# The last quarter of both MLPs' down products in seven quarter products, with part of the preparation on GpSimd

## The chip, the core and the metric

The kernel runs on one core of one Trainium2 chip. The metric is the device time of one execution, in microseconds (us); lower is better. A core has five engines with a queue of instructions each, and every queue runs strictly in its own order: TensorE (PE in the profile; its weight loads are PEld), VectorE (DVE), ScalarE (ACT), GpSimd (POOL) and SyncE (SP, which here only issues DMAs). Engines wait for each other with semaphores. All operands come from SBUF, matmuls write to PSUM.

## The reference, cut to what matters

A two-layer decoder trunk on 512 tokens of width 1024, in float32. Layer 0 mixes with latent attention, layer 1 with sliding-window attention; each layer ends with a squared-relu MLP of inner width 4096 and a layer norm:

```python
def _mlp(x, w_up, w_down):
    h = jax.nn.relu(x @ w_up)
    return (h * h) @ w_down

x = _layernorm(alpha * x + mixer(x), ln_mix_g[l], ln_mix_b[l])
x = _layernorm(alpha * x + _mlp(x, w_up, w_down), ln_mlp_g[l], ln_mlp_b[l])
```

The change is only in `(h * h) @ w_down`, and in the layer norm that follows it, in both layers.

## The kernel before, in words

**Precision.** Every operand of a large product is held as two float32r tiles, a high part (ACT copies the value, line 77) and a low part (value minus high part, line 80, on DVE by default or on POOL). A product is three matmuls: high by high, high by low, low by high (`three`, line 108). A 128-row chunk of weights, 128 x 1024, so costs one DMA of 512 KB, one ACT instruction for `wh` and one low part `wl`.

**The stream of weights.** Line 112's `stream` lists all chunks in the order of their use. `weights` (line 307) hands out one chunk and prepares others up to four ahead, since the tags `wh` and `wl` have four buffers each. SP issues the DMAs in stream order.

**Seven products.** An up or down product of one block (1024 of the 4096 inner columns) is a 2 x 2 block product of quarters. `queue_seven` (line 166) and `Block` (line 715) do it with seven quarter products in place of eight, in the manner of Strassen and Winograd; products carry the numbers 1 to 7. The combinations of weights are made by DMA: product 1's quarter is loaded by SP (line 203), and once both parts of it are made, POOL issues a DMA that adds the next quarter onto the same tile (line 199). One tile (tag `quada` for down) so goes through products 1, 5, 6 and 4 in this order, another (`quadb`) through 3 and 7; product 2 has a plain load. Each tile has two halves. The combinations of activations are made by `Factors.sum` (line 618) on DVE, and `factor` (line 792) splits each into two parts in a tile of tag `fac`, three buffers. `u2` holds two 128 x 512 sums of products 1 and 6 that several outputs need; `take` and `add_plain` (lines 712 and 562) apply them to the residual tiles `xs` at the end.

**A down product** (`down_`, line 803) takes two token tiles t of 128 tokens, and per tile four inner chunks of three matmuls of 128 x 512: 24 matmuls a product.

**The order of the work** is written out by hand in line 39's `STEPS`: U stands for up, D for down, the prime for the next block. Blocks 0 to 2 run in this way. The last block (index 3, `NFF - 1`) has its up products in seven, but its down product is plain: `LAST_STEPS` (line 40) ends with D4 of block 2, then lines 857 to 877 make four factors and call `TokMajor.finish` (line 477). That does the left 512 columns of all four tiles, inner chunk by inner chunk, then the right 512 columns tile by tile: 24 matmuls a tile, and behind each the eviction, the layer norm (line 415: DVE statistics, POOL's power for the reciprocal root at line 398, two DVE instructions of 128 x 1024) and, in layer 0, the transposes of finished tiles (`turn_tokens`, line 430) for the next stage. Its eight chunks of weights are plain loads (line 277). Layer 0 goes on with `begin` (line 579), layer 1 writes the output (line 428).

A scheduler sets the order on DVE, ACT and POOL, except where `pe` and `pin` keep the program's order. PE keeps it throughout.

Of the kernel before, what the change touches and what calls it, by code (L numbers as in the profile page):

```python
# [9 lines left out]
F32R = mybir.dt.float32r  # L10
# [5 lines left out]
P = 128  # L16
D = 1024
# [7 lines left out]
NFF = 4  # L25
# [11 lines left out]
ON_POOL = ("w_h", "w_o", "w_sq", "w_so")  # L37

STEPS = "U'1 D5 U'2 D3 U'5 D6 D7 U'3 D4 U'6 U'7 U'4 D'1 D'2"
FIRST_STEPS, LAST_STEPS = "U'1 U'2 U'5 U'3 U'6 U'7 U'4 D'1 D'2", "U'1 D5 U'2 D3 U'5 D6 D7 U'3 U'6 U'7 U'4 D4"  # L40

AHEAD_S, AHEAD_B = 3, 2

# [5 lines left out]
def build(tc, nc, io, out):  # L49
    with ExitStack() as top:  # L50
# [112 lines left out]

        mlp_pool = [None]

        def queue_seven(name, key, chunk):

# [17 lines left out]
            def grown(a, jp, *more, aside=None):  # L185
                wh, wl = tiles_of_weights(aside)
                after = None
                if aside:
                    after = state.pop("plain", None)
                elif (key, a, jp, bool(more)) == ("U", "b", 0, True):  # L190
                    after = state.get("s4")
                elif (key, a, more) == ("U", "a", (1, 0)):
                    after = state.pop(("s2", jp), None)
                with behind(after):
                    state["last"] = split(
                        wh, wl, flat(half(a, jp)), keep=(a, bool(more)) == ("b", True) and key == "U"
                    )
                if more:
                    nc.gpsimd.dma_start(half(a, jp), chunk(*more, jp), accum_op=ALU.add)  # L199
# [81 lines left out]
        for m in range(2):  # L281
# [278 lines left out]
            pin(nc.vector.scalar_tensor_tensor(xs[t][:, c], xs[t][:, c], ALPHA, b, ALU.mult, ALU.add))  # L560

        def add_plain(t, c, b):
            nc.vector.tensor_add(xs[t][:, c], b, xs[t][:, c])  # L563

        def add_scaled_last(t, c, b):
            add_scaled(t, c, b)
# [41 lines left out]
        class Factors:  # L608

            def __init__(self, mp):
                self.mp = mp

            def scratch(self):
                return self.mp.tile([P, 4, 256], F32, tag="uv", bufs=3, name=nm("uv"))

            def sum(self, n, a11, a12, a21, a22):
                if n == 5:
                    self.a = self.scratch()  # L620
                    nc.vector.tensor_sub(self.a, a21, a22)
                    return self.a
                if n == 3:
                    nc.vector.tensor_sub(self.a, self.a, a11)
                    self.b = self.scratch()
                    nc.vector.tensor_add(self.b, a12, self.a)
                    return self.b
                if n == 7:
                    nc.vector.tensor_sub(self.b, a11, a21)
# [67 lines left out]
        def mlp(src, gb, dst, mp):  # L697
# [12 lines left out]
            own_bank = {1: 1, 2: 1, 5: 5, 7: 7, 4: 7, 6: 6}  # L710

            def take(t, c, b):
                nc.vector.tensor_sub(xs[t][:, c], xs[t][:, c], b)

            class Block:
                def __init__(self, q):
                    self.q = q
                    self.g = {}
                    self.banks = {}
                    self.down = Factors(mp)  # L720
                    self.fac = {}

                def bank(self, key, i):
# [65 lines left out]
                            nc.scalar.activation(self.g[done], self.g[done], AF.Square)  # L789


                def factor(self, n, quad=False):
                    if quad:
                        f = mp.tile([P, 2, 4, 256], F32R, tag="quada", bufs=1, name=nm("fac"))
                    else:
                        f = mp.tile([P, 2, 4, 256], F32R, tag="fac", bufs=3, name=nm("fac"))
                    g = [self.g.get(a) for a in ("a11", "a12", "a21", "a22")]
                    pair = split(f[:, 0], f[:, 1], g[2] if n == 0 else self.down.sum(n, *g))
                    if (self.q, n) == (0, 1):
                        state["f1"] = state["first"] = pair  # L800
                    self.fac[n] = f

                def down_(self, n):
                    w = [weights("down") for _ in range(2)]
                    f = self.fac.pop(n)
                    key = {3: 5}.get(n) or own_bank[n]
                    for t in range(2):
                        tk = slice(t * P, (t + 1) * P)
                        b = self.bank(("D", key), t)
                        for m in range(4):  # L810
                            wh, wl = w[m // 2]
                            c = slice(m % 2 * 512, (m % 2 + 1) * 512)
                            group(
                                b, three(f[:, 0, m, tk], f[:, 1, m, tk], wh[:, c], wl[:, c]),
                                n not in (2, 3, 4) and m == 0, m == 3, skip_group_check=True,
                            )
                        add = add_scaled if self.q == 0 else add_plain
                        if n == 1 and self.q == 0:
                            nc.vector.tensor_copy(u2[t], b)
                        elif n in (1, 6):  # L820
                            nc.vector.tensor_add(u2[t], b, u2[t])
                        elif n == 2:
                            add(t, lows, b)
# [10 lines left out]
            steps = list(steps_of())  # L834

            at = {}
            for i, (which, q, n) in enumerate(steps):
                if which == "D":

                    i_q = steps.index(("U", q, {1: 6, 2: 2}.get(n, 4)))  # L840
                    i_last = steps.index(("U", q + 1, {2: 2, 3: 2}.get(n, 6))) - 1

                    at.setdefault(i_q if (q, n) == (0, 1) else max(min(i - 2, i_last), i_q), []).append((q, n))
            for i, (which, q, n) in enumerate(steps):
# [12 lines left out]
            gb = gb()  # L857
            b = blocks[NFF - 1]
            b.factor(2)
            b.factor(1)  # L860
            b.factor(4)
            b.factor(0, True)

            class Hidden:
                def h(self, k, cols):
                    return self.of(0, k, cols)

                def l(self, k, cols):
                    return self.of(1, k, cols)

                def of(self, p, k, cols):
                    n = ((2, 1), (4, 0))[cols.start // 256][k // 4]
                    return b.fac[n][:, p, k % 4, cols.start % 256 : cols.start % 256 + P]

            if dst is not None:
                state["hold"] = first_v
            TokMajor(Hidden(), add_last, "down").finish(gb, dst, dst and (0, 0, 0, 1))


        ed = dr.tile([SQH, BANDW], F32, name="ed")  # L880
# [638 lines left out]
```

## Time and profile before

| what | value |
|---|---|
| median of 3 runs (lowest to highest) | 997.25 us (997.22 to 997.62) |
| span of the profiled execution | 997.4 us |
| PE busy | 986.3 us, 99% |
| DVE busy | 771.9 us, 77% |
| ACT busy | 554.7 us, 56% |
| POOL busy | 216.5 us, 22% |
| read from HBM | 146.41 MB |

The profile covers one execution. Its page has the span and the busy times of the engines, and the trace behind it answers which instruction ran when and what ended a wait. The profiled execution's time is its span, as far as the page shows it. A busy time of a matmul is its latency, not its share of the engine: matmuls overlap, so their pace is read from starts or from the chain that ended last. "wl<-wq,wh" is a tile written by its inputs; L80 is line 80.

### The profile page before, as it was taken

What the parts mean: (1) busy time and instruction counts of PE and PEld (TensorE: products, weight loads), DVE (VectorE), ACT (ScalarE), POOL (GpSimd) and SP (SyncE); (2) the same over time, 40 slices, a digit from 0 to 9 for tenths busy, and PEclk for the clock granted to TensorE, in tenths of its full rate; (3) what the DMA queues carried; (4) which work ended last, traced back from release to release, by engine and by line L of the source; (5) the groups of instructions that cost most, each with busy time, mean ns of one, the idle gap of its engine ahead of it and who ended that gap; (6) DMA issues with size and microseconds to landing.
All of it is one profiled execution on the core that took longest, in us unless ns stands there. A gap on an engine that the chain in (4) does not pass through costs nothing.

```text
span 997.4 us, 15835 instructions
## 1 busy us (share of the span) xinstructions
PE 986.3 (99%) x6107; PEld 890.0 (89%) x6107; DVE 771.9 (77%) x1243; ACT 554.7 (56%) x850; POOL 216.5 (22%) x203
## 2 busy tenths in 40 slices
PE   9999999999999999999999999999999999999997
PEld 8988888998999999998898998889998999999986
DVE  5589967989778769877586778698985986898756
ACT  5457643467537637636145888546763664664620
POOL 0231101122212211210002775212131122123000
PEclk9999999999999999999999999999999999999999
DMA  7431126389879977963232212259798798798422
GB/s 249 143 89 54 64 106 224 92 174 243 157 171 241 175 174 202 230 118 125 87 106 96 85 65 75 96 158 208 195 187 187 166 214 175 162 263 147 117 93 85
DMA packets 60679, 149.55 MB, mean 150 GB/s; under 512 B 5260, under 2 KB 10301, under 8 KB 60605
## 3 DMA queue, kind: packets, MB, share of 16 engines
q0 software_dynamic: 24320, 58.73, 32.9%
q1 hardware_dynamic: 36140, 89.56, 27.1%
q8 instruction: 48, 0.79, 0.3%
q10 hardware_dynamic: 144, 0.26, 0.1%
q14 instruction: 27, 0.21, 0.1%
HBM read 146.41 MB, written 4.22 MB: 151 GB/s over the span
## 4 chain that ended last, share of the span: by engine, by line
PE 96%; DVE 2%; ACT 1%; DMA 1%; issue 0%; POOL 0%; DVEq 0%; SPq 0%; ACTq 0%
PE mm L104 88%; PE tr L104 5%; PE tr L1159 1%; PE tr L663 1%; PE tr L1348 1%; ACT wh L77 1%; PE tr L1350 0%; DMA raw<-in_w_kv 0%; PE tr L437 0%; DMA raw<-in_w_h 0%; DVE mm L1320 0%; DVE ptl L80 0%; PE tr L924 0%; DVE ql L80 0%; POOL wl L80 0%
## 5 line engine op out<-in xcount | busy, mean ns | idle before, releaser
L104 PE MATMUL mm<-wh,fac 128*128 128x512 f32 (+1 forms) x944 | 292.8, 387 | 0.0
L77 ACT ACTIVATE wh<-wq 128x1024 fp32r<-128x1024 f32 x164 | 173.6, 1060 | 183.6 <-PE mm L104 131.4
L80 DVE TENSOR_TENSOR wl<-wq,wh 128x1024 fp32r<-128x1024 f32 x164 | 199.7, 1222 | 70.9 <-ACT wh L77 70.1
L104 PE MATMUL mm<-xth,wh 128*128 128x256 f32 (+1 forms) x928 | 243.7, 291 | 0.0
L104 PE MATMUL mm<-xth,wl 128*128 128x256 f32 (+1 forms) x800 | 233.5, 292 | 0.0
L104 PEld LDWEIGHTS mm<-wh,fac 128*128 128x128 f32 x944 | 176.3, 188 | 35.4 <-DVE fac L80 0.6
L104 PE MATMUL mm<-xtl,wh 128*128 128x256 f32 (+1 forms) x672 | 197.4, 294 | 0.0
L104 PE MATMUL mm<-wl,fac 128*128 128x512 f32 (+1 forms) x472 | 182.4, 387 | 0.0
L104 PEld LDWEIGHTS mm<-xth,wh 128*128 128x128 f32 x928 | 168.9, 192 | 3.1
L104 PEld LDWEIGHTS mm<-xth,wl 128*128 128x128 f32 x800 | 153.4, 192 | 2.6
L77 ACT ACTIVATE wh<-raw 128x1024 fp32r<-128x1024 f32 (+3 forms) x86 | 85.0, 989 | 95.1 <-PE mm L104 56.4
L199 POOL DMA_DIRECT2D wq<-in_up x64 | 77.5, 1228 | 257.7 <-DVE wl L80 189.0
L104 PEld LDWEIGHTS mm<-xtl,wh 128*128 128x128 f32 x672 | 128.9, 192 | 3.0
L80 DVE TENSOR_TENSOR wl<-raw,wh 128x1024 fp32r<-128x1024 f32 (+2 forms) x66 | 77.1, 1174 | 35.1 <-ACT wh L77 34.7
L104 PEld LDWEIGHTS mm<-wl,fac 128*128 128x128 f32 x472 | 88.9, 188 | 16.6
L199 POOL DMA_DIRECT2D wq<-in_down x48 | 42.0, 875 | 187.5 <-DVE wl L80 181.6
L80 POOL TENSOR_TENSOR wl<-raw,wh 128x1024 fp32r<-128x1024 f32 (+2 forms) x20 | 41.2, 2063 | 87.6 <-ACT wh L77 81.9
L104 PE MATMUL mm<-wh,oh 128*128 128x512 f32 x128 | 50.9, 398 | 0.0
L104 PE MATMUL mm<-wh,ol 128*128 128x512 f32 x128 | 50.2, 392 | 0.0
L104 PE MATMUL mm<-wl,oh 128*128 128x512 f32 x128 | 50.0, 390 | 0.0
L398 POOL TENSOR_TENSOR rs<-mv,half 128x1 f32<-128x1 f32 x16 | 11.0, 689 | 167.2 <-DVE mv L419 167.1
L563 DVE TENSOR_TENSOR x<-mm,x 128x512 f32<-128x512 f32 (+1 forms) x49 | 32.9, 676 | 14.5 <-PE mm L104 14.5
(217 smaller groups left out, 1822.3 us busy)
## 6 DMA issues: line engine op xcount, KB each, us to landing
wq<-in_up POOLq DMA_DIRECT2D x64, 512.0 KB, 8.5
wq<-in_down POOLq DMA_DIRECT2D x48, 512.0 KB, 7.1
wq<-in_up SPq DMA_DIRECT2D x32, 512.0 KB, 7.0
raw<-in_down SPq DMA_DIRECT2D x28, 512.0 KB, 6.8
wq<-in_down SPq DMA_DIRECT2D x24, 512.0 KB, 5.4
raw<-in_up SPq DMA_DIRECT2D x16, 512.0 KB, 4.6
raw<-in_w_o SPq DMA_DIRECT2D x8, 512.0 KB, 4.2
raw<-in_w_sq SPq DMA_DIRECT2D x8, 512.0 KB, 3.3
```

The costliest lines, as they stand in the source:

```text
L77: high = nc.scalar.activation(dst_h, src, AF.Copy)
L80: low = (engine or nc.vector).tensor_sub(dst_l, src, f32(dst_h))
L104: pe(nc.tensor.matmul(dst, st, mv, start=first and i == 0, stop=last and i == len(pairs) - 1, **kw))
L199: nc.gpsimd.dma_start(half(a, jp), chunk(*more, jp), accum_op=ALU.add)
L398: nc.gpsimd.tensor_tensor(r, v, half, ALU.pow)
L563: nc.vector.tensor_add(xs[t][:, c], b, xs[t][:, c])
L663: pe(nc.tensor.transpose(pt[:, a, :], xs[t][:, k * P : (k + 1) * P], ident))
L1159: pe(nc.tensor.transpose(pt[:, kb * P : (kb + 1) * P], p[:, kb * P : (kb + 1) * P], ident))
L1348: pe(nc.tensor.transpose(pt[:, a, 0:P], p[:, kb, P:256], ident))
```

## The change

The plain down product of the last block becomes seven quarter products as well, in both layers. `LAST_STEPS` gains `D'1 D'2 D'5 D'6 D'3 D'7 D'4`. The first four run as whole products; product 3 is done tile by tile, each of its two tiles followed by its layer norm, and products 7 and 4 alternate: 7 and 4 of tile 2 with its layer norm, then 7 and 4 of tile 3. For this block alone, POOL takes the sums of `Factors.sum`, the low parts of the weights of products 3, 4, 6 and 7, and the six final uses of `u2`, which move from behind D6 of block 2 to behind D6 of block 3. The eight plain loads go. Product 6's sum may now be made ahead of product 3's. The prefetch of the next stage's first weights is held back to two chunks after product 7 of tile 3, and one more after the last norm.

```diff
-FIRST_STEPS, LAST_STEPS = "...", "U'1 D5 U'2 D3 U'5 D6 D7 U'3 U'6 U'7 U'4 D4"
+LAST_STEPS = "U'1 D5 U'2 D3 U'5 D6 D7 U'3 U'6 U'7 U'4 D4 D'1 D'2 D'5 D'6 D'3 D'7 D'4"
...
-                        wh, wl, flat(half(a, jp)), keep=(a, bool(more)) == ("b", True) and key == "U"
+                        wh, wl, flat(half(a, jp)), nc.gpsimd if on_pool and last_on_pool(a, more) else None,
+                        keep=(a, bool(more)) == ("b", True) and key == "U",
...
+            def last_on_pool(a, more):
+                return a == "b" or more in ((), (1, 0))
...
-            add |= {("D", q): queue_seven("down", "D", down(q)) for q in range(NFF - 1)}
+            add |= {("D", q): queue_seven("down", "D", down(q), q == NFF - 1) for q in range(NFF)}
...
-            for c in range(8):
-                queue("down", io["down"][l, (NFF - 1) * 8 + c])
...
-                    self.down = Factors(mp)
+                    self.down = Factors(mp, nc.gpsimd if q == NFF - 1 else nc.vector)
...
-                    if (q, n) == (NFF - 2, 6):
+                    if (q, n) == (NFF - 1, 6):
                         for t in range(2):
-                            take(t, highs, u2[t])
-                            take(2 + t, highs, u2[t])
-                            add_plain(2 + t, lows, u2[t])
+                            nc.gpsimd.tensor_sub(xs[t][:, highs], xs[t][:, highs], u2[t])
+                        for t in range(2):
+                            nc.gpsimd.tensor_sub(xs[2 + t][:, highs], xs[2 + t][:, highs], u2[t])
+                            nc.gpsimd.tensor_add(xs[2 + t][:, lows], xs[2 + t][:, lows], u2[t])
...
+            w, f = last.operands(3)
+            for t in range(2):
+                out_of(add_last, t, highs, last.product(3, t, w, f))
+                norm(t)
+            (w7, f7), (w4, f4) = last.operands(7), last.operands(4)
+            for t in range(2):
+                out_of(take_last, 2 + t, highs, last.product(7, t, w7, f7))
+                if dst is not None and t == 1:
+                    prepare(2)
...
+                else:
+                    out_of(add_last, 2 + t, lows, last.product(4, t, w4, f4))
+                norm(2 + t)
```

`norm(t)` is the layer norm of tile t; in layer 0 it also queues the transposes of the tile before it. `product` is the body of `down_` for one tile. In layer 1 the last product of tile 3 is done in two halves of 256 columns.

More of the change, by code (lines that the diff above doesn't have):

```diff
@@ L164, in build, with queue_seven @@
         mlp_pool = [None]
-        def queue_seven(name, key, chunk):
+        def queue_seven(name, key, chunk, on_pool=False):
             quads = {}
@@ L562, in add_plain @@
         def add_plain(t, c, b):
-            nc.vector.tensor_add(xs[t][:, c], b, xs[t][:, c])
+            pin(nc.vector.tensor_add(xs[t][:, c], b, xs[t][:, c]))
         def add_scaled_last(t, c, b):
@@ L608, in build, with __init__ @@
         class Factors:
-            def __init__(self, mp):
+            def __init__(self, mp, engine=None):
                 self.mp = mp
+                self.engine = engine or nc.vector
             def scratch(self):
@@ L620, in sum @@
                     self.a = self.scratch()
-                    nc.vector.tensor_sub(self.a, a21, a22)
+                    self.engine.tensor_sub(self.a, a21, a22)
+                    self.whole = False
                     return self.a
+                if n in (3, 6) and not self.whole:
+                    self.engine.tensor_sub(self.a, self.a, a11)
+                    self.whole = True
                 if n == 3:
-                    nc.vector.tensor_sub(self.a, self.a, a11)
                     self.b = self.scratch()
-                    nc.vector.tensor_add(self.b, a12, self.a)
+                    self.engine.tensor_add(self.b, a12, self.a)
                     return self.b
                 if n == 7:
-                    nc.vector.tensor_sub(self.b, a11, a21)
+                    self.engine.tensor_sub(self.b, a11, a21)
                     return self.b
@@ L712, in take @@
             def take(t, c, b):
-                nc.vector.tensor_sub(xs[t][:, c], xs[t][:, c], b)
+                pin(nc.vector.tensor_sub(xs[t][:, c], xs[t][:, c], b))
             class Block:
@@ L789, in up_out, with factor @@
                             nc.scalar.activation(self.g[done], self.g[done], AF.Square)
[L792 to L796, printed above, removed]
+                def factor(self, n):
+                    f = mp.tile([P, 2, 4, 256], F32R, tag="fac", bufs=3, name=nm("fac"))
                     g = [self.g.get(a) for a in ("a11", "a12", "a21", "a22")]
-                    pair = split(f[:, 0], f[:, 1], g[2] if n == 0 else self.down.sum(n, *g))
+                    pair = split(f[:, 0], f[:, 1], self.down.sum(n, *g))
                     if (self.q, n) == (0, 1):
@@ L801, in factor, with product, operands @@
                     self.fac[n] = f
+                def product(self, n, t, w, f, fresh=None, cols=lows):
+                    tk = slice(t * P, (t + 1) * P)
+                    b = fresh or self.bank(("D", {3: 5}.get(n) or own_bank[n]), t)
+                    for m in range(4):
+                        wh, wl = w[m // 2]
+                        c = slice(m % 2 * 512 + cols.start, m % 2 * 512 + cols.stop)
+                        group(
+                            b, three(f[:, 0, m, tk], f[:, 1, m, tk], wh[:, c], wl[:, c]),
+                            (fresh or n not in (2, 3, 4)) and m == 0, m == 3, skip_group_check=True,
+                        )
+                    return b
+                def operands(self, n):
+                    return [weights("down") for _ in range(2)], self.fac.pop(n)
                 def down_(self, n):
-                    w = [weights("down") for _ in range(2)]
-                    f = self.fac.pop(n)
-                    key = {3: 5}.get(n) or own_bank[n]
+                    w, f = self.operands(n)
                     for t in range(2):
[L808 to L816, printed above, removed]
+                        b = self.product(n, t, w, f)
                         add = add_scaled if self.q == 0 else add_plain
@@ L822, in down_ @@
                         elif n == 2:
-                            add(t, lows, b)
+                            (add_last if self.q == NFF - 1 else add)(t, lows, b)
                         elif n == 5:
@@ L834, in mlp @@
             steps = list(steps_of())
+            last = blocks[NFF - 1]
             at = {}
@@ L840, in mlp, with norm, out_of, take_last @@
                     i_q = steps.index(("U", q, {1: 6, 2: 2}.get(n, 4)))
-                    i_last = steps.index(("U", q + 1, {2: 2, 3: 2}.get(n, 6))) - 1
+                    i_last = len(steps)
+                    if q < NFF - 1:
+                        i_last = steps.index(("U", q + 1, {2: 2, 3: 2}.get(n, 6))) - 1
                     at.setdefault(i_q if (q, n) == (0, 1) else max(min(i - 2, i_last), i_q), []).append((q, n))
-            for i, (which, q, n) in enumerate(steps):
+            def norm(t):
+                pinned[0] = True
+                with tc.high_priority():
+                    layer_norm(t, gb, dst)
+                if dst is not None and t == NT - 1:
+                    prepare(1)
+                pinned[0] = False
+                if dst is not None and t in (1, 2):
+                    with tc.high_priority():
+                        dst.turn(t - 1)
+            def out_of(f, *what):
+                pinned[0] = True
+                with tc.high_priority():
+                    f(*what)
+                pinned[0] = False
+            def take_last(t, c, b):
+                take(t, c, b)
+                count(t, c)
+            for i, (which, q, n) in enumerate(steps[:-3]):
                 if which == "U":
@@ L857, in mlp @@
             gb = gb()
[L858 to L873, printed above, removed]
-            if dst is not None:
-                state["hold"] = first_v
-            TokMajor(Hidden(), add_last, "down").finish(gb, dst, dst and (0, 0, 0, 1))
+            last.factor(4)
+            if dst is not None:
+                state["hold"] = first_v - 2
+            w, f = last.operands(3)
[7 more added lines that the diff above has]
+                    prepare(2)
+                if dst is None and t == 1:
+                    out_of(add_plain, 3, lows, last.bank(("D", 7), t))
+                    for c in (slice(0, 256), slice(256, 512)):
+                        out_of(add_last, 3, c, last.product(4, t, w4, f4, bank(256), c))
+                else:
+                    out_of(add_last, 2 + t, lows, last.product(4, t, w4, f4))
+                norm(2 + t)
         ed = dr.tile([SQH, BANDW], F32, name="ed")
```

2 lines of the change are left out of this document (1 added, 1 removed).

## The prediction

> **What bounds the kernel now.** I read the engines' busy times and shares of the last chain first, then the chain in order of time, then both stretches that change.
>
> ```profile
> span 997.4 us, 15835 instructions
> PE 986.3 (99%) x6107; PEld 890.0 (89%) x6107; DVE 771.9 (77%) x1243; ACT 554.7 (56%) x850; POOL 216.5 (22%) x203
> PE 96%; DVE 2%; ACT 1%; DMA 1%; issue 0%; POOL 0%; DVEq 0%; SPq 0%; ACTq 0%
> ```
>
> ```profile
> 446.96 49.80 PE mm L104 x264
> 496.76 0.87 PE tr L437 x8
> 497.63 5.46 PE mm L104 x24
> 503.10 0.87 PE tr L437 x8
> 503.97 11.22 PE mm L104 x72
> ...
> 929.05 61.00 PE mm L104 x336
> ...
> 993.86 0.40 DVE x L425
> ```
>
> TensorE is the bound: 96% of the chain, and no other engine shows more than 2%. Between the transposes, 24 matmuls of one tile take 5.46 us. That is the price of a matmul of 512 columns, 0.2275 us. The first MLP's last tile ends at 503.97 + 5.46 = 509.4, the second's at about 990.
>
> ```profile
> 463.98 0.69 DVE L563 TENSOR_TENSOR x<-mm,x 128x512 f32<-128x512 f32 x1 [0.62 <-PE mm L104]
> 946.07 0.69 DVE L563 TENSOR_TENSOR x<-mm,x 128x512 f32<-128x512 f32 x1 [1.53 <-PE mm L104]
> ```
>
> These evictions end D4 of block 2, so the last block's down product starts at about 463.7 and 945.8. The stretches from there to its end:
>
> ```profile
> 463.70:509.40 45.70, 45.70 (x212) 37.81 (x211) 29.68 (x42) 11.32 (x13) 2.75 (x3) 1.00 0.31 94
> 945.80:989.90 44.10, 44.10 (x218) 37.21 (x216) 27.31 (x38) 6.37 (x6) 1.65 (x3) 1.00 0.26 93
> ```
>
> After the length come the busy times of PE, PEld, DVE, ACT and POOL. POOL has 2.75 us of work in 45.7 us. That is the room the change goes into; how long its own operations take decides.
>
> **TensorE's part.** 192 matmuls become 7 x 24 = 168: 24 fewer, 5.46 us in each MLP, 10.9 us if nothing waits. The stretch would be 40.2 us.
>
> **POOL's part.**
>
> ```profile
> L199 POOL DMA_DIRECT2D wq<-in_down x48 | 42.0, 875 | 187.5 <-DVE wl L80 181.6 <-DVE x L560 5.9
> L80 POOL TENSOR_TENSOR wl<-raw,wh 128x1024 fp32r<-128x1024 f32 x12 | 28.7, 2398 | 54.4 <-ACT wh L77 51.3 <-PE mm L104 3.0
> L80 POOL TENSOR_TENSOR ol<-o,oh 128x512 fp32r<-128x512 f32 x8 | 10.8, 1351 | 12.0 <-ACT oh L77 12.0
> L1337 POOL TENSOR_TENSOR p<-p,ri 128x768 f32<-128x768 f32 x16 | 23.5, 1467 | 0.0
> 499.00 0.55 POOL L398 TENSOR_TENSOR rs<-mv,half 128x1 f32<-128x1 f32 x1 [4.24 <-DVE mv L419]
> wq<-in_down POOLq DMA_DIRECT2D x48, 512.0 KB, 7.1
> L80 DVE TENSOR_TENSOR wl<-wq,wh 128x1024 fp32r<-128x1024 f32 x164 | 199.7, 1222 | 70.9 <-ACT wh L77 70.1
> L77 ACT ACTIVATE wh<-wq 128x1024 fp32r<-128x1024 f32 x164 | 173.6, 1060 | 183.6 <-PE mm L104 131.4
> ```
>
> Per MLP POOL gets eight low parts at 2.40 (19.2), four sums of the same width, eight accumulating DMAs at 0.875 (7.0, landing 7.1 after issue) and six uses of `u2` of 512 columns at 1.3 (7.8). No row shows a POOL sum from f32 to f32 of 1024 columns. The 768-wide row scales to 1.96, the low part gives 2.40; I take 2.40, the same width (4 x 2.4 = 9.6), and the lower end saves 1.8 us an MLP. With two reciprocal roots (1.1) that is 44.7 us ahead of product 7 of tile 3, in a stretch of 40.2.
>
> The order in which the compiled kernel queues it on POOL: two DMAs for product 5, sums 5, 6 and 3, two DMAs for 6, low part 6a, sum 7, DMA 4a, low parts 6b, 3a, 3b, DMAs 4b and 7a, three uses of `u2`, DMA 7b, three uses, root of tile 0, low parts 7a, 7b, 4a, 4b, root of tile 1. Each waits for all ahead of it.
>
> **When POOL can start.** Product 1's load needs `quada`, whose last reader is a low part:
>
> ```profile
> 454.69 1.23 DVE L80 TENSOR_TENSOR wl<-wq,wh 128x1024 fp32r<-128x1024 f32 x1 [0.34 <-ACT wh L77]
> 935.87 1.22 DVE L80 TENSOR_TENSOR wl<-wq,wh 128x1024 fp32r<-128x1024 f32 x1 [0.34 <-ACT wh L77]
> 462.28 1.06 ACT L789 ACTIVATE a<-a 128x1024 f32<-128x1024 f32 x1
> wq<-in_down SPq DMA_DIRECT2D x24, 512.0 KB, 5.4
> ```
>
> Free at 455.9, landed at 461.4 and 461.9. ACT makes both high parts first (to 463.6), and only then the square that ended at 463.3 before: 465.7 now. So sum 5 starts at 465.9, behind DMAs 5a and 5b. **A floor** follows even if POOL never waits again: 465.9 + 44.7 - 1.75 = 508.9, then the second norm instruction of tile 1 (1.28), the transposes (0.87) and 24 matmuls (5.46): 516.5 against 509.4. The PE saving is already in it. It is 7.1 us late per MLP, whatever DVE does.
>
> **What POOL and DVE do to each other.**
>
> ```profile
> 638.43 1.81 POOL L80 TENSOR_TENSOR ol<-o,oh 128x512 fp32r<-128x512 f32 x1 [6.48 <-ACT oh L77]
> 637.87 1.23 DVE L80 TENSOR_TENSOR wl<-raw,wh 128x1024 fp32r<-128x1024 f32 x1 [1.17 <-ACT wh L77]
> 639.34 1.98 DVE L80 TENSOR_TENSOR wl<-raw,wh 128x1024 fp32r<-128x1024 f32 x1 [0.25 <-ACT wh L77]
> ```
>
> The POOL instruction took 1.81 in place of 1.28 at its quickest, as if it began its work when DVE's first low part ended; the next DVE one took 1.98 in place of 1.22, as if it waited for POOL's end. I read this as: DVE's two-input work on SBUF and POOL's work exclude each other. The Trainium skill says so in "SBUF — State Buffer", section "Who interferes with whom": of a two-SBUF-input DVE operation and a GpSimd operation on SBUF, the first to start holds the port for its whole instruction. The rule agrees with these three rows and speaks against this change, which puts both streams side by side; with it the sum is 1048, without it 1032.
>
> **Replay of the first MLP** by these durations, with exclusion. Sum 5 465.9-468.3; DVE's low parts 2a, 2b to 470.6, factor 5's low part to 472.4; sum 6 to 474.8 (it overwrites sum 5, so it waits for that low part); low part 5a to 476.0; sum 3 to 478.4; DMA 6a is queued behind it and lands at 485.5; high part at 486.6, low part 6a to 489.0; sum 7 to 491.4, DMA, low part 6b to 494.6; DVE's factor 7 to 495.8; low parts 3a, 3b to 500.6; two DMAs and three uses of `u2` to 506.3; DVE's first norm instruction of tile 0 to 507.5; three uses to 511.4; root of tile 0 at 512.0; low part 7a to 514.4; second norm instruction to 515.6; 7b to 518.0; DVE to 519.2; 4a, 4b to 524.0; root of tile 1, its norm instruction to 525.8; transposes 526.7; 24 matmuls: 532.2. Against 509.4 that is **+22.8**.
>
> Costs at nothing: six more high parts and three more factors on ACT (9.5 us more, beside POOL's waits; ACT stays under half of the stretch). DVE gives away work.
>
> Behind it, the next stage's first low part waits for tile 3's norm:
>
> ```profile
> 514.81 1.22 DVE L80 TENSOR_TENSOR wl<-raw,wh 128x1024 fp32r<-128x1024 f32 x1
> ```
>
> Before it ended 6.6 us after the product (516.03), just in time. Now tile 2's norm and prefetched low parts stand closer ahead of it: I take 8.7, **+2.1**; bounds 0 and 5.
>
> **Second MLP.** `quada` is free at 937.1, 0.9 us earlier against its stretch. The same replay puts low part 4b at 945.8 + 60.3 - 0.9 = 1005.2, product 4 of tile 2 at 1006.6, the last 24 matmuls at 1012.1. Tile 2's norm starts only at 1006.6 and waits on the same port; with tile 3's behind it DVE ends at 1020.3. Before, the last instruction started at 993.86, ended near 994.3, and the span closed 3.1 later: 1023.4, **+26.0**.
>
> **Sum:** 997.4 + 22.8 + 2.1 + 26.0 = 1048.3, so 1048. The span is the profiled execution's time; the median of the runs, 997.25, is the same within 0.2%, about 2 us, which is what a measurement of this kernel can tell from no change.
>
> **Rivals.**
>
> 1. *No exclusion, or a light one* (the 1.98 had another reason). The chain is then ordered by queue alone: the same replay with both engines free ends at 524.5 (+15.1) and 17.6 later in the second, +2: **1032**, span 1018 to 1038. For it: only one overlap of this kind is clean. Against: both engines slowed there, by amounts that fit one waiting for the other.
>
> 2. *POOL never waits*: the floor, 2 x 7.1 behind PE's end, and less with sums of 1.96: **1003 to 1018**. Against: DMA 6a, queued behind sum 3, takes 7.1 to land while low part 6a stands at the head of POOL's queue.
>
> 3. *PE's clock falls in the gaps.* PE idles some 8 us in the replay ahead of products 6, 3 and 7. The only long idle time of this trace is its start:
>
> ```profile
> 8.03 1.27 PE L104 MATMUL mm<-wl,xth 128*128 128x320 f32 x4
> 9.10 0.92 PE L104 MATMUL mm<-wh,xth 128*128 128x320 f32 x4
> 9.86 0.74 PE L104 MATMUL mm<-wh,xtl 128*128 128x320 f32 x4
> 10.44 0.75 PE L104 MATMUL mm<-wl,xth 128*128 128x320 f32 x4
> ```
>
> Groups of four start 1.07, 0.76 and 0.58 apart: 0.7 us lost until full speed. With three such gaps an MLP, if all are on the path, 4 us: **1052**. The Trainium skill's "TensorE: Matmul & The Clock Gate", "Part 1: The HAM clock gate", would have it so: after an idle window of some 3.4 us the PE runs at half rate until it was busy as long. An estimate from that page is up to 1.7 us a gap.
>
> 4. *PE stays the bound, faster.* Everything on POOL hides, and only the wait of tile 0's transposes is left:
>
> ```profile
> 491.35 0.69 DVE L563 TENSOR_TENSOR x<-mm,x 128x512 f32<-128x512 f32 x1 [2.24 <-PE mm L104]
> 494.80 1.28 DVE L425 SCALAR_TENSOR_TENSOR x<-x,rs,gb 128x1024 f32<-128x1024 f32 x1 [0.46 <-POOL rs L398]
> ```
>
> From eviction to normed tile are 4.7 us, while product 7 is not begun and product 3 of tile 1 gives cover of 2.7: 2 us lost, 997.4 - 10.9 + 2.2 = **988.7**. It decides at POOL's wide operation: twelve of them must fit between 465.9 and 495.9 (product 4 of tile 2) beside 13.5 us of DMAs, uses and roots, so at 1.37 us or less. Twelve rows of this trace have 2.40 as their mean. Only if the sums and low parts ran far quicker here would it come.
>
> 5. *Harsher*: POOL's wide instructions wait for DVE's two-input work too, as the 1.81 row did. If each of the twelve waits half a DVE low part (0.6), 7 us more an MLP: **1062**, and up to twice that. Against: in the replay DVE is mostly the one that waits.
>
> **Chances.** Replay with exclusion (1038 to 1060) 36%, the same with PE's slow restarts (1040 to 1060) 10%, light exclusion (1018 to 1038) 30%, POOL without waits (1003 to 1018) 8%, of which 5% above 1012, above 1060 8%, faster 5%, within 0.2% 3%. So faster 5%, same 3%, slower 92%. The range 1012 to 1060 leaves out 19%.
>
> **What would show it.** POOL busy without gaps in both stretches, some 45 us where 2.75 were; its low parts 2.4 or longer; DVE low parts of 2 to 4 us beside it. PE idle ahead of product 6 (by low part 6a), 3 and 7, and the transposes of tile 1 waiting for a norm that waits for a root. The first MLP's product ends near 532, the second's near 1012. I am wrong if POOL's instructions of 1024 columns take near 1.4, if the root of tile 0 isn't late, or if PE shows no gap over 1 us in the stretches.

## The result, and the profile after

| | us |
|---|---|
| before, median of 5 (lowest to highest) | 997.62 (997.22 to 998.19) |
| after, median of 5 (lowest to highest) | 1042.17 (1042.01 to 1053.79) |
| ratio | 1.0469, 95% interval 1.0446 to 1.0492 |
| forecast | 1048, range 1012 to 1060 |

The change made the kernel 4.7% slower. Its executions fall into two groups, near 1042 and near 1052, and the one with the first profile (span 1051.8) is of the second group; a second profile, from the run `e0_again` below, has a span of 1039.8 and is of the first. Both are used, and each number says from which it is.

The page of after, 1051.8, with span, engines and shares of the chain that ended last:

```profile
span 1051.8 us, 15831 instructions
PE 991.5 (94%) x6047; PEld 888.8 (85%) x6047; DVE 825.0 (78%) x1246; ACT 573.5 (55%) x868; POOL 303.9 (29%) x255
PE 86%; DVE 8%; POOL 2%; issue 2%; DMA 1%; ACT 1%; DVEq 0%; SPq 0%; POOLq 0%
```

PE's share of the chain fell from 96% to 86%, DVE's rose from 2% to 8%, POOL's to 2%. POOL has 52 instructions more, the 26 an MLP of the forecast, and PE 60 fewer recorded (48 matmuls by count; some records are missing), so the change does what it says. The windows of the first MLP's last block, from D4 of block 2 to the end of the product (columns as in the prediction), first in after, then in `e0_again`:

```profile
462.06:535.40 73.34, 48.78 (x186) 38.10 (x185) 60.73 (x49) 20.95 (x24) 43.64 (x27) 0.81 0.45 98
```

```profile
461.66:526.20 64.54, 46.94 (x186) 36.42 (x185) 49.73 (x49) 20.86 (x23) 45.76 (x27) 0.87 0.50 113
```

45.7 us became 73.3 and 64.5. POOL is busy 44 to 46 us, where the forecast had 45. In the chain of after, in order of time, the longest piece of this stretch is one DVE instruction (pieces under 0.3 us left out):

```profile
488.40 7.00 PE mm L105 x17
495.42 1.07 ACT fac L78
496.52 1.67 DVE fac L81
498.32 0.69 DVE x L566
499.03 0.70 DVE bn L556
500.01 14.89 DVE x L425
514.99 1.29 DVE x L428
516.33 1.97 PE tr L440 x8
518.30 4.46 PE mm L105 x12
```

The first norm instruction of tile 0 takes 14.89; the one of tile 1 that follows took 1.31 (517.88). Behind it stand the second norm instruction, the transposes of tile 0 and, on PE, all that follows. What POOL did in that time (timelines of DVE and POOL, after):

```profile
486.29 7.79 DVE L81 TENSOR_TENSOR fac<-uv,fac 128x1024 fp32r<-128x1024 f32 x1 [3.22 <-ACT fac L78]
500.01 14.88 DVE L425 SCALAR_TENSOR_TENSOR x<-x,mv,gb 128x1024 f32<-128x1024 f32 x1
...
517.88 1.31 DVE L425 SCALAR_TENSOR_TENSOR x<-x,mv,gb 128x1024 f32<-128x1024 f32 x1
```

```profile
485.71 7.28 POOL L81 TENSOR_TENSOR wl<-wq,wh 128x1024 fp32r<-128x1024 f32 x3
...
500.10 1.57 POOL L885 TENSOR_TENSOR x<-x,u 128x512 f32<-128x512 f32 x1
501.34 1.55 POOL L887 TENSOR_TENSOR x<-x,u 128x512 f32<-128x512 f32 x1
502.56 1.54 POOL L888 TENSOR_TENSOR x<-x,u 128x512 f32<-128x512 f32 x1
503.78 0.83 POOL L401 TENSOR_TENSOR rs<-mv,half 128x1 f32<-128x1 f32 x1
504.32 9.47 POOL L81 TENSOR_TENSOR wl<-wq,wh 128x1024 fp32r<-128x1024 f32 x4
```

Factor 7's low part on DVE ends (494.08) 1.1 us after POOL's run of three low parts (492.99), and the norm instruction (514.89) 1.1 us after the run of three uses, root and four low parts (513.79). That is about its own length (1.2 to 1.3): DVE waited for a whole unbroken run. By the records the norm instruction began 0.09 us ahead of that run and waited all the same. The group at 1042 shows the same with another outcome (`e0_again`, DVE, then POOL):

```profile
498.19 1.88 DVE L425 SCALAR_TENSOR_TENSOR x<-x,mv,gb 128x1024 f32<-128x1024 f32 x1
504.20 3.38 DVE L428 SCALAR_TENSOR_TENSOR x<-x,rs,gb 128x1024 f32<-128x1024 f32 x1 [4.13 <-POOL rs L401]
507.50 0.68 DVE L566 TENSOR_TENSOR x<-mm,x 128x512 f32<-128x512 f32 x1
```

```profile
499.53 1.65 POOL L885 TENSOR_TENSOR x<-x,u 128x512 f32<-128x512 f32 x1
...
503.60 0.56 POOL L401 TENSOR_TENSOR rs<-mv,half 128x1 f32<-128x1 f32 x1
504.14 11.34 POOL L81 TENSOR_TENSOR wl<-wq,wh 128x1024 fp32r<-128x1024 f32 x4
515.44 0.55 POOL L401 TENSOR_TENSOR rs<-mv,half 128x1 f32<-128x1 f32 x1
```

There the first norm instruction came 1.8 us earlier, ahead of the second three uses (from 499.53), and took 1.88; the second one waited for one low part only (3.38). Now POOL's four low parts last 11.3 us, and tile 1's root stands behind them. The eviction from PSUM at 507.50 took 0.68 in the middle of that run: one of its two inputs is in PSUM, and it took no longer than beside an idle POOL.

### The profile page after: what moved, and what is told of

Read it like the earlier page. It is cut to its first block, busy times and chain, and to the rows that moved or that the text cites. A ratio compares the mean times of both kernels' runs of the same rounds, so it can differ in the third digit from the quotient of the medians.

```text
span 1051.8 us, 15831 instructions
## 1 busy us (share of the span) xinstructions
PE 991.5 (94%) x6047; PEld 888.8 (85%) x6047; DVE 825.0 (78%) x1246; ACT 573.5 (55%) x868; POOL 303.9 (29%) x255
## 4 chain that ended last, share of the span: by engine, by line
PE 86%; DVE 8%; POOL 2%; issue 2%; DMA 1%; ACT 1%; DVEq 0%; SPq 0%; POOLq 0%
PE mm L105 78%; PE tr L105 4%; DVE x L425 3%; DMA wq<-in_down 1%; POOL wl L81 1%; DVE wl L81 1%; PE tr L1193 1%; PE tr L670 1%; DVE x L428 1%; PE tr L1382 1%; DVE fac L81 1%; DVE bn L556 0%; POOL uv L633 0%; DVE x L566 0%; POOL uv L629 0%
## 5 line engine op out<-in xcount | busy, mean ns | idle before, releaser
L78 ACT ACTIVATE wh<-wq 128x1024 fp32r<-128x1024 f32 x188 | 198.2, 1059 | 224.9 <-PE mm L105 134.5
L81 DVE TENSOR_TENSOR wl<-wq,wh 128x1024 fp32r<-128x1024 f32 x172 | 210.6, 1229 | 79.8 <-ACT wh L78 78.8
L201 POOL DMA_DIRECT2D wq<-in_down x64 | 56.5, 901 | 234.3 <-DVE wl L81 231.7
L78 ACT ACTIVATE wh<-raw 128x1024 fp32r<-128x1024 f32 (+3 forms) x74 | 72.4, 978 | 62.5 <-PE mm L105 39.2
L81 DVE TENSOR_TENSOR wl<-raw,wh 128x1024 fp32r<-128x1024 f32 (+3 forms) x54 | 64.0, 1197 | 12.5 <-ACT wh L78 12.2
L81 DVE TENSOR_TENSOR fac<-uv,fac 128x1024 fp32r<-128x1024 f32 x32 | 55.2, 1726 | 8.5 <-ACT fac L78 8.5
L425 DVE SCALAR_TENSOR_TENSOR x<-x,mv,gb 128x1024 f32<-128x1024 f32 x16 | 48.1, 3009 | 0.6
```

Source lines behind the costliest of these rows:

```text
L78: high = nc.scalar.activation(dst_h, src, AF.Copy)
L81: low = (engine or nc.vector).tensor_sub(dst_l, src, f32(dst_h))
L425: pin(nc.vector.scalar_tensor_tensor(x, x, mv[:, 0:1], gb[0], ALU.subtract, ALU.mult))
```

## The experiments

Theory A: DVE's instructions with two SBUF inputs and POOL's work exclude each other, and POOL can keep DVE out over a whole unbroken run. Rivals: one instruction only (B), POOL's queue alone (C), PE's slow restarts on the path (D). Times are medians unless single executions are listed; the kernel before was measured again beside each run (medians 997.2 to 997.5).

**The change again** (no edit).

> The changed kernel once more, unchanged: its executions so far were 1042.0 to 1043.4 with one of 1053.8, and the one with a profile was the 1053.8. Theory A (a DVE instruction with two SBUF inputs that finds POOL at work waits until POOL's whole unbroken run of instructions is over): an execution near 1042 has the same waits, with one of the two long ones (14.9 us at the first norm instruction of tile 0) some 6 us shorter in each MLP, because DVE slips in earlier. Theory B (it waits for one POOL instruction only): no wait on DVE over 3.5 us in such an execution. Theory C (POOL's queue alone sets the end, the waits of DVE lie beside it): the roots of tiles 0 and 1 and low part 4b end at the same times, whatever DVE waits. Time 1042 by all three.

Measured: 1041.74, 1042.45, 1051.37, 1051.95. Theory A's two outcomes are those shown above, but the first norm instruction is 13 us shorter here, where some 6 were expected. B fails: factor 7's low part took 7.65 in this profile too, and 7.57 to 7.81 in both MLPs of all six traces in which POOL makes three low parts in a row there (after, `e0_again`, `e3_takes_dve`, `e5_warm`, `e6_low74_dve`, `e8_pause`). C fails as well: low part 4b ends 51.7 us into the stretch in the 1052 group and 53.8 into it in the 1042 group, yet the product ends at 73.3 and at 64.5. POOL was through earlier in the slower execution; what came later was DVE's norm.

**One part after the other back to DVE.** Three switches: the eight low parts (`last_on_pool`), the sums, the uses of `u2`.

```diff
-                return a == "b" or more in ((), (1, 0))
+                return False
...
-                    self.down = Factors(mp, nc.gpsimd if q == NFF - 1 else nc.vector)
+                    self.down = Factors(mp)
...
-                            nc.gpsimd.tensor_sub(xs[t][:, highs], xs[t][:, highs], u2[t])
+                            nc.vector.tensor_sub(xs[t][:, highs], xs[t][:, highs], u2[t])
```

(and the other two uses likewise; `e1_low_dve` has the first edit, `e3_takes_dve` the third, `e4_all_dve` all).

> The eight low parts of products 6, 3, 7 and 4 go back to DVE, sums and uses of u2 stay on POOL. POOL loses 19 us an MLP, DVE gains 9.8. Theory A: the run of four low parts behind the root of tile 0 is gone, and with it most of the 14.9 us; what is left is DVE's own length: some 4 us an MLP over the kernel before, 1006 in all. Theory B: 1000, as each wait is of one use or sum only. Theory C: POOL's queue is through by some 490 in the first MLP, so PE is the bound again: 988 to 992.

> The six uses of u2 go to DVE, the rest stays on POOL. POOL loses 7.8 us an MLP, DVE gains 4.2. Theory A: the run behind which the first norm instruction of tile 0 waits is now the root and four low parts, so the wait starts and ends earlier by the 7.8 us at most: 1042 less 2 x 7 = 1028. Theory B: the uses were in the chain one by one: 1042 less 2 x 5.7 = 1031. Theory C: 1042 less 2 x 7.8 = 1026.

> All three parts go back to DVE: seven quarter products with only the accumulating DMAs and roots on POOL. DVE gets some 21 us more in each stretch than the kernel before had (29.7 us busy in 45.7), so 50 us in a stretch of 40 for PE. All theories: no long wait of DVE for POOL is left; DVE's length is the bound, some 3 us an MLP over the kernel before: 1003; if DVE can take part of it ahead of the stretch, 990.

Three more runs have one part alone on POOL (the sums with the first and third edits, the low parts with the second and third, the uses with the first and second):

> Seven products with only the four sums on POOL; low parts and uses of u2 on DVE. The kernel with all three on DVE took 1020.7, and there DVE has no idle time over 2 us between 463 and 504 us; with sums and uses on POOL it took 1028.1. Theory I (POOL and DVE share one port, so what DVE gives away at 1.2 us comes back as 2.4 us of waiting): half of the 7.4 between these two, about 1024. Theory J (DVE is the bound, so each part given to POOL is a gain, and what costs is only where POOL's queue makes DMAs late): 2 x 4.6 us less than 1020.7, 1012.

> Seven products with only the eight low parts on POOL; sums and uses of u2 on DVE. All three on DVE took 1020.7; low parts and sums on POOL 1045.1. Theory I (one port for both): DVE gives away 9.2 us and gets up to 19.2 us of waiting an MLP, 1020.7 + 2 x 10 = 1040. Theory J: the queue on POOL is shorter by sums and uses, DVE by 9.2 us: 1005.

> Seven products with only the six uses of u2 on POOL, the rest on DVE. Theory I: DVE gives away 3.6 us and meets 7.8 us of POOL work, part of it beside DVE's work on PSUM: 1024. Theory J: 2 x 3.6 less than 1020.7, 1014, unless the accumulating DMAs of product 7 come to stand behind the uses, as in the changed kernel.

| on POOL | us | against none |
|---|---|---|
| nothing (`e4_all_dve`) | 1020.67 (1019.45 to 1020.84) | |
| uses (`e11_takes_only_pool`) | 1025.36 (1023.89 to 1026.54) | +4.7 |
| sums (`e9_sums_only_pool`) | 1026.10 (1023.95 to 1027.88) | +5.4 |
| sums and uses (`e1_low_dve`) | 1028.09 (1025.98 to 1030.76) | +7.4 |
| low parts (`e10_low_only_pool`) | 1032.09 (1031.98 to 1033.01) | +11.4 |
| low parts and sums (`e3_takes_dve`) | 1045.05 (1042.32 to 1045.45) | +24.4 |
| all, the change | 1042.17 and the group at 1052 | +21.5, +31 |

No part pays on POOL. Each alone makes the kernel slower than with all on DVE; beside another part it does so too, but for the uses beside the two others in the group at 1042. Sums and uses together lie 2.0 and 2.7 above one of them alone, with ranges that overlap, and low parts with uses weren't run. Low parts and sums together cost more than one by one (24.4 against 16.8). Theory J falls (its 1012, 1005 and 1014 stand at 1026, 1032 and 1025); theory I has the sign in all three, and 8 us too much for the low parts. Other numbers were wrong in size: `e1_low_dve` by 22 against theory A, `e3_takes_dve` by 17 (taking the uses off POOL saved nothing: DVE now does them ahead of tile 0's eviction, which began at 501.76 in place of 496.50), `e4_all_dve` by 18. The last is the largest finding: with no part on POOL the seven products still lose 23 us. The window of its stretch:

```profile
461.80:521.30 59.50, 43.70 (x185) 34.10 (x185) 52.96 (x67) 20.59 (x24) 6.80 (x9) 0.91 0.53 121
```

DVE is busy for 53.0 of 59.5 us (29.7 of 45.7 before), in a stretch for which PE needs 40.2. PE's order, DVE's length, or DVE's own order with the DMAs behind it can make PE wait.

**Another order on PE**, with all three parts on DVE:

```diff
             for t in range(2):
                 out_of(take_last, 2 + t, highs, last.product(7, t, w7, f7))
-                if dst is not None and t == 1:
-                    prepare(2)
+            if dst is not None:
+                prepare(2)
+                for t in range(2):
+                    with tc.high_priority():
+                        dst.turn(t)
+            for t in range(2):
```

(the transposes leave their old places; in layer 1 only the order of the products changes).

> The kernel with all three parts on DVE (1020.7), with another order on PE: product 7 of tiles 2 and 3, then the transposes of tiles 0 and 1, then product 4 of tiles 2 and 3. There, 10.0 us of PE's gaps in the first MLP stand ahead of the transposes of tile 0, and 3.2 between products 7 and 4, which share a bank. Theory G (PE's order is what is left): 6 us less in the first MLP and 4 in the second, 1010. Theory H (DVE's length is what is left, any order on PE waits for it elsewhere): 1017 or more.

Measured: 1020.59 (1020.11 to 1021.39), as without it. PE's waits moved (rows of PE that waited, new order):

```profile
508.69 1.97 PE L440 MATMUL tr<-ident,x 128*128 128x128 f32 x8 [6.49 <-DVE x L428]
514.09 1.94 PE L440 MATMUL tr<-ident,x 128*128 128x128 f32 x8 [3.43 <-DVE x L428]
```

In place of 10.0 us ahead of tile 0's transposes come 6.5 and 3.4 ahead of both tiles', each behind a norm instruction on DVE. Theory G falls, and theory H's number holds. That DVE's length is all that is left isn't shown by it, since DVE takes tile 0's eviction late in both runs. In `e4_all_dve` (ACT, then DVE):

```profile
494.39 2.95 ACT L78 ACTIVATE wh<-wq 128x1024 fp32r<-128x1024 f32 x3 [1.40 <-DMA wq<-in_down]
```

```profile
495.48 2.36 DVE L81 TENSOR_TENSOR wl<-wq,wh 128x1024 fp32r<-128x1024 f32 x2 [1.07 <-ACT wh L78]
497.76 0.68 DVE L566 TENSOR_TENSOR x<-mm,x 128x512 f32<-128x512 f32 x1
```

Tile 0's eviction began at 497.76, behind low parts of products 7 and 4 that waited for a DMA (at 499.05 in the run with the new order, behind the same low parts), though product 3 of tile 0 had ended near 490.5 (an estimate: PE's last matmul of tile 1 ended at 493.25, less 12 matmuls of 0.2275). Of the 59.5 us DVE was idle for 6.5, of which 3.2 were spent on ACT's copies of weights. No run puts this eviction first on DVE.

**Only the low parts of products 7 and 4 on DVE.**

```diff
-                return a == "b" or more in ((), (1, 0))
+                return (a == "b" and more) or more == (1, 0)
```

> Only the four low parts of products 7 and 4 go back to DVE; those of 6 and 3, the sums and the uses of u2 stay on POOL. Theory E (the last four low parts and the root behind them set the end): tile 1's root no longer stands behind 9.5 us of POOL work, some 4 us less an MLP: 1034, and no execution near 1052. Theory F (what counts is POOL's work ahead of the root of tile 0): 1040 or more. The kernel with all eight low parts on DVE took 1028.

Measured: 1042.70 (1041.04 to 1045.34); theory E falls. Theory F's number holds, but not by its path: tile 0's root waited for DVE here. The trace shows what took the place of the run of four: DMA 7b is queued on POOL behind three uses, so ACT's high parts are late, and with them the low parts on DVE, ahead of tile 0's eviction (POOL, ACT, DVE):

```profile
499.19 0.87 POOL L201 DMA_DIRECT2D wq<-in_down  x1
```

```profile
504.77 2.95 ACT L78 ACTIVATE wh<-wq 128x1024 fp32r<-128x1024 f32 x3 [3.11 <-DMA wq<-in_down]
```

```profile
505.86 2.36 DVE L81 TENSOR_TENSOR wl<-wq,wh 128x1024 fp32r<-128x1024 f32 x2 [0.98 <-ACT wh L78]
508.13 0.68 DVE L566 TENSOR_TENSOR x<-mm,x 128x512 f32<-128x512 f32 x1
```

In `e0_again` that eviction of tile 0 began at 496.50.

**A pause on POOL**: one column of tile 0 is copied on POOL, and the preparation of products 7 and 4 is held back until then.

```diff
                 norm(t)
+                if t == 0:
+                    mark = sp.tile([P, 1], F32, tag="mark", bufs=2, name=nm("mark"))
+                    pause = nc.gpsimd.tensor_copy(mark, xs[0][:, 0:1])
...
+            with tc.issue_after(pause.ins):
+                (w7, f7), (w4, f4) = last.operands(7), last.operands(4)
```

> The changed kernel with a pause on POOL: a copy of one column of tile 0 behind its norm stands ahead of low parts 7a, 7b, 4a and 4b, so POOL leaves DVE alone until tile 0 is normed. Theory A (DVE can be held for POOL's whole unbroken run; the executions at 1052 are those in which the first norm instruction of tile 0 was caught by the run of three uses, root and four low parts): no execution above 1046, and 1042 +- 3 in the median, since the low parts start some 3 us later and wait less for DVE. Theory B (the 1052 come from something else, the DMAs or the clock): executions near 1042 and near 1052 both appear again.

Measured: 1048.78, five executions from 1047.82 to 1050.69. Neither theory's number: all five lie above A's 1046, and B's two groups don't show. One group fits theory A, and in this profile the two norm instructions of tile 0 took 1.84 and 1.28; but three of the nine executions of the change so far were of the group at 1052, so that five in one group would come by chance about one time in eight. The level is 6.6 above 1042, where 3 were allowed. By the two profiles (spans 1046.3 and 1039.8) 2.0 us of it arise in the first MLP's stretch and 0.4 in the second, about what was expected of low parts that start later; 2.8 and 1.4 arise ahead of the two stretches, where the pause adds no instruction, and stay unexplained.

**40 more matmuls ahead of tile 0's transposes**, so that PE doesn't idle there.

```diff
                 pinned[0] = False
+                if t == 1:
+                    spare = bank()
+                    for _ in range(40):
+                        group(spare, [(f[:, 0, 0, 0:P], w[0][0][:, 0:512])])
```

(in `norm`, ahead of the transposes).

> The changed kernel with 40 more matmuls (their result is not used) on PE ahead of the transposes of tile 0, 9.1 us at full rate, in the gap of 8.8 to 15.5 us. Theory D (PE's slow restart behind this gap is on the path: transposes 1.97 in place of 1.03, three groups of three matmuls 1.28 in place of 0.68): 2.7 us less an MLP, 1037, or 1047 in the other group of executions. Theory E (slow PE lies beside POOL's four low parts, and only the end of those and the root behind them count): the groups show full rate, and the time stays at 1042 within 1.5 us.

Measured: 1050.26 (1049.35 to 1051.79). Neither theory's number. PE did keep full speed (transposes 1.03 for 1.97), product 7 of tile 2 ended at 511.8, and then PE waited for DVE, longer than before:

```profile
508.03 1.03 PE L440 MATMUL tr<-ident,x 128*128 128x128 f32 x8
518.01 0.77 PE L105 MATMUL mm<-wh,fac 128*128 128x512 f32 x1 [6.19 <-DVE x L720]
```

```profile
513.91 3.36 DVE L428 SCALAR_TENSOR_TENSOR x<-x,rs,gb 128x1024 f32<-128x1024 f32 x1 [1.57 <-POOL rs L401]
517.19 0.68 DVE L720 TENSOR_TENSOR x<-x,mm 128x512 f32<-128x512 f32 x1
```

Here root 1 stood ahead of low part 4b, so tile 1's norm instruction met that low part (3.36), with the eviction of product 7 queued behind it. The gain of theory D didn't come: the faster PE only waited longer for DVE. As POOL's order changed too, the run doesn't price the restart by itself.

**The kernel before with its own eight low parts on POOL**, products plain.

```diff
-                queue("down", io["down"][l, (NFF - 1) * 8 + c])
+                queue("down", io["down"][l, (NFF - 1) * 8 + c], nc.gpsimd)
```

> The kernel before (plain last block) with the eight low parts of its last block on POOL, one for each 5.5 us of PE's work, in both layers. Theory I in its simplest form (a low part on POOL costs what it is longer, wherever it stands): 8 x 1.2 us an MLP, 1016. Theory K (work on POOL costs only where DVE or PE has no slack; here DVE is idle 3 to 4 us ahead of each of the low parts): 998 to 999, at most the root of tile 0 late behind the last low part.

Measured: 1000.54 (999.49 to 1001.03), ratio 1.0032 (1.0021 to 1.0044). Nearer to K than to I, and above K's number. The later low parts, beside an idle DVE, make nothing wait in this trace, but the early ones meet the last factors' low parts, 3.13 and 2.58 for 1.22, and PE waits for one of them, 1.15 us and in the second MLP 1.46 (DVE, PE):

```profile
458.93 3.13 DVE L80 TENSOR_TENSOR fac<-a,fac 128x1024 fp32r<-128x1024 f32 x1 [1.23 <-ACT fac L77]
...
464.12 2.58 DVE L80 TENSOR_TENSOR fac<-a,fac 128x1024 fp32r<-128x1024 f32 x1 [0.86 <-ACT fac L77]
```

```profile
466.76 0.73 PE L104 MATMUL mm<-wh,fac 128*128 128x512 f32 x2 [1.15 <-DVE fac L80]
```

No run beat the kernel before.

## Why the prediction was right, point by point

The sum against `e0_again`, whose execution stands for the median:

| term | forecast | 1042 group | 1052 group |
|---|---|---|---|
| start of the first stretch | 0 | -2.0 | -1.6 |
| first MLP | +22.8 | +18.8 | +27.6 |
| between the MLPs | +2.1 | +0.9 | -0.2 |
| second MLP to the end | +26.0 | +24.7 | +28.6 |
| sum | +50.9 | +42.4 | +54.4 |

The first MLP is 64.54 or 73.34 less 45.70. The other terms come from the spans and the evictions that end D4 of block 2 in the second MLP, 0.28 behind the stretch's start as in the first (`e0_again`, then after):

```profile
963.78 0.69 DVE L566 TENSOR_TENSOR x<-mm,x 128x512 f32<-128x512 f32 x1 [1.33 <-PE mm L105]
```

```profile
971.87 0.69 DVE L566 TENSOR_TENSOR x<-mm,x 128x512 f32<-128x512 f32 x1 [1.28 <-PE mm L105]
```

1. **POOL's work, its order and its price** were right: 45.8 us busy in the stretch of `e0_again` against 44.7, low parts at 2.3 to 2.4 where nothing held them. That POOL would be busy without gaps was wrong: the stretch is 64.5.
2. **When POOL can start** was too late (ACT, then POOL, after):

```profile
456.75 1.06 ACT L78 ACTIVATE wh<-wq 128x1024 fp32r<-128x1024 f32 x1
458.05 1.06 ACT L78 ACTIVATE wh<-wq 128x1024 fp32r<-128x1024 f32 x1 [0.23 <-DMA wq<-in_down]
```

```profile
461.24 2.72 POOL L625 TENSOR_TENSOR uv<-a,a 128x1024 f32<-128x1024 f32 x1
```

   Product 1's loads had landed by 456.75 and 458.05, 5.3 and 4.0 us ahead of the stretch, where the forecast had 2.3 and 1.8. So sum 5 began 0.8 ahead of the stretch's start and not 2.2 behind it. The accumulating DMAs also landed sooner, 5.5 us after issue (median in `e0_again`) and not 7.1. So the later steps of the replay were too late as well: the root of tile 0 ended 42.5 us into the stretch in `e0_again` (forecast 48.3), low part 4b 53.8 (60.3). The first MLP's term was too high by 4.0 us, less than these steps, since points 5 and 7 work the other way.
3. **Exclusion** was right as a mechanism, and the chain ran over it. The Trainium skill's rule ("SBUF — State Buffer", "Who interferes with whom") agrees in who excludes whom; its unit, the whole instruction, was exceeded here: 7.79 us for three instructions, 14.88 for eight. This term was too small in the 1052 group: the replay let DVE in behind each POOL instruction.
4. **Rival 1** (1032, no exclusion) is out: DVE waited for POOL's whole runs. **Rival 2** (1003 to 1018, POOL's queue as the floor) is out too, and not the only floor: without any of those parts on POOL it is 1020.7. **Rival 5** was right that POOL waits as well (sum 3 took 3.25, two low parts 3.34 and 3.38 in `e0_again`), but the time stayed below its 1062.
5. **Rival 3**: slow restarts came, and 0.7 us a gap was too low a price. It was read from 8.03 us on, but the groups that start at 5.74 and 6.97 (1.23 and 1.06 apart, 0.58 at full speed) were slow already. In the chain of after, 17 matmuls behind a gap of 3.88 take 7.00, where 17 times 0.2275 are 3.9, and the eight transposes with 12 matmuls behind the gap of 15.48 take 6.4, where 0.87 + 2.73 are 3.6: some 3 us each (an estimate from these rows), and both are on the chain. The 40 matmuls took the second away without gain; the first wasn't tried.
6. **Rival 4's decision point left DVE out.** I wrote that PE stays the bound if POOL's wide operation took 1.37 us. On DVE these operations take 1.22 us, and the time is still 23 us above before: "DVE gives away work" hid that the change first adds 13 operations of 1.22 (six low parts, three factors' low parts, four sums: 15.9 us) to DVE's side of the account, and six uses that had been done ahead of the stretch. So 23 of the 44.6 us come with none of these parts on POOL, and 21.5 with putting them there. DVE's 53.0 us of work alone make 7.3 of the 13.8 us by which the stretch of `e4_all_dve` exceeds 45.7; how the rest divides among DVE's order, the DMAs and PE's restarts isn't shown. The forecast put all of it on POOL; its total was near because the work of either engine exceeds PE's 40.2 us.
7. **Missed altogether**: product 4 of a tile adds onto the PSUM bank of its product 7, so it waits for the eviction of product 7, 0.87 and 2.07 us in the first MLP of `e0_again`. The next stage's +2.1 was too much by 1.2.
8. **The number owes something to luck.** Terms that were too high (point 2) and terms left out or too small (points 3, 5 and 7) offset each other, and 1048 lies between two groups that the replay didn't foresee. The sum is also built on a span, and an execution of the change lasts some 2 us longer than its span (1041.74 and 1039.8): against the span it is 8.5 too high, against the median of the times 6. The direction and the mechanism don't hang on this.

## What to carry to other kernels

Fewer products are worth having only where the engines that prepare them have room in that same stretch: add up the preparation by engine there, on the best engine first, before looking at where to put it. Work given to POOL isn't simply taken from DVE if both read SBUF: here each 1.2 us of DVE became 2.4 us of POOL, for which DVE's two-input instructions were seen to wait. And an in-order queue makes the DMA issues and roots behind such work late as well, so a part taken back doesn't always give its time back.

## What the runs showed of the hardware

- DVE held by POOL over whole runs (7.79, 14.88 us; 7.65 in `e0_again`), and in `e0_again` also over one instruction of a run of four (3.38). What decides isn't settled. In the long wait POOL's records overlap by 0.3 us (1.57 long, 1.24 apart), in the short one hardly.
- PE's restart. Rows of after behind the gap of 15.48 us, and after a gap of 1.72:

```profile
518.95 1.05 PE L105 MATMUL mm<-wh,fac 128*128 128x512 f32 x2
...
524.15 0.62 PE L105 MATMUL mm<-wh,fac 128*128 128x512 f32 x2
```

```profile
476.61 0.50 PE L105 MATMUL mm<-wl,fac 128*128 128x512 f32 x1 [1.72 <-DVE wl L81]
476.94 0.62 PE L105 MATMUL mm<-wh,fac 128*128 128x512 f32 x2
477.39 0.59 PE L105 MATMUL mm<-wl,fac 128*128 128x512 f32 x1
477.78 1.06 PE L105 MATMUL mm<-wh,fac 128*128 128x512 f32 x2
```

  The pair takes 1.05 for 0.62 for some 5 us behind the long gap; the granted clock was 0.50 from 516.3 to 521.8 and 1.00 from 521.8 on. A gap of only 1.72 us was followed by full rate first and then by 2.6 us of the slow rate (clock 0.50 from 477.7 to 480.4), while one of 2.32 us ahead of 532.54 was followed by none (1.00).
